# Block products of single chunks, with their weight sums on GpSimd, in a two-layer mLSTM and RG-LRU trunk

## The chip, the cores and the metric

The kernel runs on one core of a Trainium2 chip, in one launch. The metric is the device time of one execution in microseconds (us). Engines are named as in the profile: PE (TensorE matmul), PEld (its weight load), DVE (VectorE), ACT (ScalarE), POOL (GpSimd), SP (the queue that issues most DMAs).

## The reference

x is 256 tokens of 2048 channels, float32. Each of two layers does this; a final RMS norm follows.

```python
u = rms_norm(x, norm_g)
p = u @ w_in                               # 2048 x 12304
qk, v, o, z_a, ig, fg, xb, z_b = split(p)  # 2048 columns each, gates 8
qk = silu(causal_dwconv(qk, qk_conv))
h = mlstm_chunkwise(q, k, v, ig, fg)       # 8 heads
h = headwise_norm(h * sigmoid(o)) * head_norm_g
y_a = h * silu(z_a)
xc = causal_dwconv(xb, lru_conv_w) + lru_conv_b
y_b = rg_lru(xc, w_a, w_x, ...) * silu(z_b)   # 8 blocks of 256 x 256
x = x + concat([y_a, y_b]) @ w_out         # 4096 x 2048
```

Nearly all arithmetic is in the products with w_in and w_out; every weight is used once, for all 256 tokens.

## The kernel before

**Products in three passes.** A float32 weight is split into a high part wH (ACT casts to the float32r type) and the rest wL (DVE subtracts wH from the raw weight); activations are split likewise. A product is the sum of three matmuls: high by high, high by low, low by high. In the big products the activation (128 channels by 128 tokens) is the stationary operand and the weight, 512 columns wide, the moving one.

**Chunks, units and halves.** Columns are cut into four groups of 512 for each of qk, v, o, z, xb and zb. Such a chunk `("in", l, kind, g)` is four units, a unit two halves; a half is 128 x 1024 weights (512 KB), 2 blocks of 128 rows by 512 columns. It takes a load into `raw`, an ACT cast, a DVE subtraction (`prepare`, recorded at L114 like everything that goes through the helper `Behind`) and 12 matmuls in `mm_a` (L413). The out projection has four chunks of two units for each group; `gate` is one unit of small products (L879, 24 matmuls of 256 columns in a half).

**The order.** `_sequence` writes out the items of a layer group by group; the main loop walks the halves in that order. It loads into 8 buffers of `raw`, prepares halves up to `AHEAD` = 3 ahead of the matmuls (4 buffers each for wH and wL), and after each half lets the other work advance in the generators of `bg`. `pump` starts as much of it as an estimate of DVE's arrears (`st["lag"]`) allows; `require` forces it where a result is needed. `Behind` keeps other work of DVE and ACT behind the split that is due. Other work is: turning token layout into channel layout (`swapped`: a DVE transpose into `blk`, four SP transfers into `moved`, one POOL transfer back into `fr`), convolutions, attention, the recurrence, norms.

**Pairs.** In each layer two pairs of chunks (`PAIRS`: v and o of group 2; o and z of group 3) are done with seven products of blocks instead of eight: tokens, input channels and the two chunks are each halved, so that a block of weights is 1024 rows by the 512 columns of one chunk. A product is four halves of 6 matmuls of 512 columns (L1234 to L1236), in one bank of PSUM; results are put together in `res` by DVE. The 28 halves of a pair are spread between plain halves. Sums of activations are made by DVE in `sums` (`block_sums`); sums of weights are made in DRAM, by POOL transfers that copy and add (`weight_sums`, L1141), and are loaded from there; one product adds two loaded blocks on DVE.

**PSUM.** Two double banks `acc`, three single banks `aux` and one `bank` make the eight.

Of the kernel before, what the change touches and what calls it, by code (L numbers as in the profile page):

```python
# [16 lines left out]
P = 128  # L17
D = 2048
T = 256
# [8 lines left out]
AHEAD = 3  # L28
LANDING = 10.0
FAR = 15.0  # L30
BORDER = 7
BLANKS = 7
RATE = 0.9, 0.8
COPY, ADDING, TURN = 1.3, 2.6, 2.9
SLOTS = 8
SUMS_FROM = 20
# [7 lines left out]

def _sequence():


    def units(item):
        return [(item, j) for j in range(_nunits(item))]

    seq = []
    for l in range(DEPTH):
        for g in range(NG):
            fill = [("out", l, g - 1, c) for c in range(4)] if g > 0 else []
            head = {0: ("o", "qk", "v", "xb"), 1: ("qk", "o", "v", "xb"), 2: ("qk", "xb", "o", "v")}.get(g, ("qk", "v", "xb"))
            items = [("in", l, k, g) for k in head] + fill
            items += [("in", l, k, g) for k in (("o", "z") if g == NG - 1 else ("z",))] + [("gate", l, g)]
            items.insert(len(items) if g > 0 else -2, ("in", l, "zb", g))
            us = [u for it in items for u in units(it)]
            if l > 0 and g == 0:  # L60
                us[0:8] = [us[i] for i in (0, 4, 1, 5, 2, 6, 3, 7)]
            seq += us
        if l + 1 < DEPTH:
            u = [u for c in range(4) for u in units(("out", l, NG - 1, c))]
            seq += [u[i] for i in (0, 2, 1, 3, 4, 5, 6, 7)]
        else:
            seq += units(("last", l, NG - 1))
    return seq


PAIRS = (("v", NG - 2), ("o", NG - 2)), (("o", NG - 1), ("z", NG - 1))
PRODUCTS = 2, 2


def _blockwise(item):

    return item[0] == "in" and any(item[2:] in pair for pair in PAIRS[: PRODUCTS[item[1]]])

# [21 lines left out]
def tile_trunk(ctx, tc, x, xt, par, gw, gb, ws, final_g, out):  # L100
    nc = tc.nc
    G, PE = nc.gpsimd, nc.tensor
    done = {"wH": [], "wL": []}

# [15 lines left out]
    V, S = Behind(nc.vector, "wL"), Behind(nc.scalar, "wH")  # L120

    const = ctx.enter_context(tc.tile_pool(name="const", bufs=1))
    wraw = ctx.enter_context(tc.tile_pool(name="wraw", bufs=SLOTS))
    wsp = ctx.enter_context(tc.tile_pool(name="wsp", bufs=4))
# [5 lines left out]
    st = {"nload": 0, "lag": 0.0, "dma": 0.0, "t": 0.0, "rate": RATE[0], "nprep": 0, "pair": 0, "aux": 0}  # L130

    def aux(name):
        st["aux"] = (st["aux"] + 1) % 3
        return psum.tile([P, 512], F32, tag=f"aux{st['aux']}", name=name)

    def bank(name):
        return psum.tile([P, 512], F32, tag="bank", name=name)

    def new_acc():
        st["pair"] = 1 - st["pair"]  # L140
        return psum.tile([P, 2, 512], F32, tag=f"acc{st['pair']}", name="acc")
# [22 lines left out]
    def load_x_c(c):  # L164
        order(nc.sync.dma_start(out=xa(c), in_=xd[c]), st["ld"])
        st["dma"] += COPY

    def store_x(c):
        S.dma_start(out=xd[c], in_=xa(c))
        st["dma"] += COPY  # L170
# [86 lines left out]
    def lam_gen():  # L257
        lams = act.tile([P, 4, DEPTH, 16], F32, tag="res", name="lams")
# [11 lines left out]
    def order(ins, prev):  # L270
        tc.add_manual_dep(ins.ins, prev.ins.name,
                          mybir.DependencyInfo(mybir.DependencyClass.NoSync, mybir.DependencyReason.DATA),
                          reason="an order of the program")

    def paced(ins, prev):
        tc.add_manual_dep(ins.ins, prev.ins.name,
                          mybir.DependencyInfo(mybir.DependencyClass.Sync, mybir.DependencyReason.DATA),
                          reason="a transfer begun behind it")

    bg, aside = deque(), []  # L280
# [17 lines left out]
    def beside(g):  # L298
        aside.append(g)
        bg.append(g)  # L300
# [10 lines left out]
    def require(key):  # L311
        i = 0
        while key not in st:
            st["forced"] = True
            i = step(i)
# [19 lines left out]
    def load_half(hf):  # L335
        n = st["nload"]
        st["nload"] += 1
        if "from" in hf and hf["made"]:
            require(hf["made"])
        raw = hf["raw"] = wraw.tile([P, 1024], F32, tag="raw", name="raw")  # L340
        st["dma"] += COPY
        if "from" in hf:
            st["ld"] = nc.sync.dma_start(out=raw, in_=hf["from"])
            if "and" in hf:
                hf["other"] = wraw.tile([P, 1024], F32, tag="raw", name="raw")
                st["ld"] = nc.sync.dma_start(out=hf["other"], in_=hf["and"])
                st["dma"] += COPY
            return
        (item, j), i = hf["at"], hf["i"]
        if n < 8:  # L350
            w = 512 if n < 2 else 1024
            load_xt(n // 2, i)
            for o in range(0, 1024, w):
                nc.sync.dma_start(out=raw[:, o : o + w], in_=ws[blocks[item, j]][:, 1024 * i + o : 1024 * i + o + w])
        elif hf["paired"]:
# [3 lines left out]
        else:  # L359
            st["ld"] = nc.sync.dma_start(out=raw, in_=ws[blocks[item, j]][:, 1024 * i : 1024 * i + 1024])  # L360
# [3 lines left out]
    def add_unit(mms, before=None, after=None, paired=False, own=None):  # L364
        halves.append([dict(i=i, mm=mms[i], split=None, paired=paired, own=own and own[i],
# [1251 lines left out]
```

## Time and profile before

| | |
|---|---|
| median of 3 runs (lowest to highest) | 1478.68 us (1477.67 to 1482.82) |
| profiled execution, its time and its span | 1479.07 us, 1477.2 us |
| mean granted clock of TensorE | 0.999 |
| PE, DVE, ACT, POOL busy | 99%, 82%, 66%, 9% of the span |
| DMA | 417.06 MB, 282 GB/s on average |

In rows of the profile, a group of instructions is given as line, engine, operation, output<-inputs, output and input shapes, count, then busy us and mean ns of one, then the idle time of the engine before them and what ended it. A row of waits reads: who <- for whom: us in total, times, longest. A row of a timeline reads: start, length, engine, line, operation; rows of several instructions say so with x2. A row of a stretch reads: from, to, length, then busy us of an engine and the instructions in brackets. DMA rows give the count, the size and the median us from issue to landing.

### The profile page before, as it was taken

How to read it: one execution, taken by the hardware profiler on the slowest of the kernel's cores; microseconds unless marked ns; L12 is line 12 of the kernel's file. 1: busy time of each engine (PE TensorE's matmuls, PEld its weight loads, DVE VectorE, ACT ScalarE, POOL GpSimd, SP SyncE). 2: the span in 40 equal slices, each digit the busy share in tenths (PEclk: the TensorE clock that was granted, in tenths of full speed). 3: DMA queues.
4: the chain of work that ended last, by engine and by line, in shares of the span. 5: the costliest groups of instructions: out<-in, count | busy, mean ns of one | idle time of the engine just before them, and what ended most of it. 6: DMA issues, size and time to landing. Idle time of an engine off the chain costs nothing.

```text
span 1477.2 us, 19595 instructions
## 1 busy us (share of the span) xinstructions
PE 1460.8 (99%) x6734; PEld 1217.2 (82%) x6734; DVE 1213.1 (82%) x1710; ACT 981.5 (66%) x1255; POOL 129.5 (9%) x210
## 2 busy tenths in 40 slices
PE   9999999999999999999999999999999999999997
PEld 7888888888888888888888788888888788888885
DVE  6888898878888699888857789988787877998875
ACT  7666766568676666668665577655677756667774
POOL 0020110110100000100100201111000000000002
PEclk9999999999999999999999999999999999999999
DMA  9979999999989998988998888999988899888891
GB/s 343 337 242 283 284 315 292 309 252 330 348 288 257 289 335 286 303 250 285 293 301 258 229 277 275 292 299 275 316 263 295 251 261 286 307 287 269 232 342 60
DMA packets 158708, 417.06 MB, mean 282 GB/s; under 512 B 14848, under 2 KB 35344, under 8 KB 158608
## 3 DMA queue, kind: packets, MB, share of 16 engines
q1 hardware_dynamic: 136432, 340.01, 67.7%
q0 software_dynamic: 19712, 71.33, 21.1%
q10 hardware_dynamic: 2464, 4.47, 0.8%
q8 instruction: 53, 0.87, 0.2%
q14 instruction: 47, 0.39, 0.1%
HBM read 378.50 MB, written 74.99 MB: 307 GB/s over the span
## 4 chain that ended last, share of the span: by engine, by line
PE 86%; DMA 6%; DVE 4%; issue 3%; ACT 1%; SPq 0%; POOL 0%; POOLq 0%; DVEq 0%; ACTq 0%
PE acc L413 68%; PE ps_b L1234 3%; PE ps_b L1236 3%; PE ps_b L1235 3%; PE ps_gt L879 3%; DMA raw<-in_ws_dram 2%; DMA fr<-moved 2%; PE acc L426 2%; DMA moved<-blk 1%; DVE wL L114 1%; DVE xc L114 1%; DVE qc L114 1%; PE acc L1358 1%; PE acc L1359 1%; PE acc L1357 1%
## 5 line engine op out<-in xcount | busy, mean ns | idle before, releaser
L114 DVE TENSOR_TENSOR wL<-raw,wH 128x1024 fp32r<-128x1024 f32 (+1 forms) x580 | 692.8, 1202 | 187.1 <-ACT wH L114 185.2
L114 ACT CAST wH<-raw 128x1024 fp32r<-128x1024 f32 (+1 forms) x580 | 597.2, 1039 | 356.1 <-PE acc L413 250.2
L413 PE MATMUL acc<-wH,x_s 128*128 128x512 f32 x2496 | 783.7, 389 | 0.0
L413 PEld LDWEIGHTS acc<-wH,x_s 128*128 128x128 f32 x2496 | 468.3, 188 | 97.6 <-ACT wH L114 1.1
L413 PE MATMUL acc<-wL,x_s 128*128 128x512 f32 x1248 | 484.7, 389 | 3.0 <-DVE wL L114 3.0
L413 PEld LDWEIGHTS acc<-wL,x_s 128*128 128x128 f32 x1248 | 234.3, 188 | 51.9 <-DVE wL L114 4.1
L413 PE MATMUL acc<-wL,ybH 128*128 128x512 f32 x224 | 87.3, 390 | 0.6 <-DVE wL L114 0.6
L413 PE MATMUL acc<-wH,ybL 128*128 128x512 f32 x224 | 87.5, 390 | 0.3 <-DVE ybL L989 0.3
L413 PE MATMUL acc<-wH,ybH 128*128 128x512 f32 x224 | 87.6, 391 | 0.0
L413 PE MATMUL acc<-wH,yaH 128*128 128x512 f32 x224 | 87.4, 390 | 0.0
L413 PE MATMUL acc<-wL,yaH 128*128 128x512 f32 x224 | 87.2, 389 | 0.0
L413 PE MATMUL acc<-wH,yaL 128*128 128x512 f32 x224 | 87.2, 389 | 0.0
L114 ACT ACT_TABLE_LOAD x62 | 79.5, 1283 | 5.1 <-DVE qc L114 2.7
L1141 POOL DMA_DIRECT2D w_d<-in_ws_dram x64 | 48.9, 765 | 292.8 <-ACT wH L114 265.4
L536 POOL DMA_DIRECT2D fr<-moved x34 | 19.2, 566 | 511.3 <-DMA moved<-blk 450.9
L114 DVE SCALAR_TENSOR_TENSOR xc<-ch,pars,xc 128x255 f32<-128x255 f32 (+2 forms) x96 | 42.3, 477 | 10.3 <-ACT xc L114 10.0
L1234 PE MATMUL ps_b<-wH,sums 128*128 128x512 f32 x128 | 50.1, 391 | 0.0
L413 PEld LDWEIGHTS acc<-wH,ybL 128*128 128x128 f32 x224 | 42.1, 188 | 9.7 <-DVE ybL L989 1.0
L1236 PE MATMUL ps_b<-wH,sums 128*128 128x512 f32 x128 | 49.9, 390 | 0.0
L1235 PE MATMUL ps_b<-wL,sums 128*128 128x512 f32 x128 | 49.9, 390 | 0.0
L413 PEld LDWEIGHTS acc<-wL,ybH 128*128 128x128 f32 x224 | 42.1, 188 | 9.3 <-DVE wL L114 0.9
L413 PEld LDWEIGHTS acc<-wH,yaL 128*128 128x128 f32 x224 | 42.0, 188 | 8.8
(229 smaller groups left out, 1763.2 us busy)
## 6 DMA issues: line engine op xcount, KB each, us to landing
raw<-in_ws_dram SPq DMA_DIRECT2D x542, 512.0 KB, 6.7
w_d<-in_ws_dram POOLq DMA_DIRECT2D x64, 512.0 KB, 9.1
raw<-w_d SPq DMA_DIRECT2D x48, 512.0 KB, 6.7
fr<-moved POOLq DMA_DIRECT2D x34, 512.0 KB, 7.3
moved<-blk SPq DMA_DIRECT2D x132, 128.0 KB, 3.9
x_d<-stage POOLq DMA_DIRECT2D x24, 512.0 KB, 7.9
x_d<-x_acc ACTq DMA_DIRECT2D x8, 512.0 KB, 7.8
w_d<-w_d POOLq DMA_DIRECT2D x8, 512.0 KB, 7.0
```

The costliest lines, as they stand in the source:

```text
L114: ins = f(*a, **k)
L413: st["mm"] = PE.matmul(o, a_[:, kt, P * t : P * t + P], W[:, k], start=b, stop=z)
L426: PE.matmul(ps[:, ct, T * part : 2 * T], W[:, k, P * ct : P * ct + P], moving, start=first and k == 0 and part == 0, stop=last and k == 3 ...
L536: i0 = back.dma_start(out=fr.rearrange("p a c t i -> p a (c t i)"), in_=moved)
L879: PE.matmul(o, W[:, ib, jl], xs[:, ib, a, :], start=j == 0 and i == 0 and W is Hv and a == 0, stop=i == 1 and W is Lv, skip_group_check=True)
L1141: i0 = G.dma_start(out=wd[l][p][to][j][:, cs], in_=(wd[l][p][src][j] if src == 0 else block_unit(l, p, *src, j))[:, cs], **how)
L1234: PE.matmul(box["b"], aH, Hv[:, k], start=opening and k == 0, stop=False, skip_group_check=True)
L1235: PE.matmul(box["b"], aH, Lv[:, k], start=False, stop=False, skip_group_check=True)
L1236: PE.matmul(box["b"], aL, Hv[:, k], start=False, stop=kp == 3 and k == 1, skip_group_check=True)
L1357: PE.matmul(o, yH[:, kt, tsl], Hv[:, k, cs], start=start and k == 0, stop=False)
L1358: PE.matmul(o, yH[:, kt, tsl], Lv[:, k, cs], start=False, stop=False)
L1359: PE.matmul(o, yL[:, kt, tsl], Hv[:, k, cs], start=False, stop=stop and k == 1)
```

## The change

The pairs go, with their sums in DRAM. Blockwise now are single chunks: o and v of groups 1 to 3 and z of all groups, 10 chunks in each layer. Tokens, input channels and the 512 columns of one chunk are halved, so a block of weights is 1024 rows by 256 columns. A blocked half holds 128 rows of all four blocks (4 x 256 columns). GpSimd adds three more columns blocks beside them in SBUF:

```diff
+    def weight_sums(hf):
+        lo = hf["place"][0]
+        b = raws[:, lo : lo + 1792].rearrange("p (b n) -> p b n", b=7)
+        G.tensor_tensor(out=b[:, 4:6], in0=b[:, 0:4:3], in1=b[:, 1:2].to_broadcast([P, 2, 256]), op=ALU.add)
+        G.tensor_tensor(out=b[:, 6], in0=b[:, 4], in1=b[:, 3], op=ALU.add)
+        G.tensor_tensor(out=b[:, 1], in0=b[:, 6], in1=b[:, 2], op=ALU.add)
```

ACT and DVE then split 1792 columns, and the half does 7 products of 3 matmuls of 256 columns, for all seven block products at once, in two double banks that the chunk holds from its first half to its last:

```diff
+    def mm_s(l, box, kt):
...
+            for A, w, bank, at in ((x(0, 0), 0, a[:, 0], 0), (x(0, 1), 2, a[:, 1], 0), (s(1), 6, a[:, 1], 1),
+                                   (s(2), 5, b[:, 0], 0), (s(0), 4, b[:, 0], 1),
+                                   (s(3), 3, b[:, 1], 0), (x(1, 1), 1, b[:, 1], 1)):
+                o, cs = bank[:, 256 * at : 256 * at + 256], slice(256 * w, 256 * w + 256)
+                aH, aL = A()
+                PE.matmul(o, aH, H[:, cs], start=kt == 0 and at == 0, stop=False, skip_group_check=True)
+                PE.matmul(o, aH, L[:, cs], start=False, stop=False, skip_group_check=True)
+                st["mm"] = PE.matmul(o, aL, H[:, cs], start=False, stop=kt == 7, skip_group_check=True)
```

Behind the last half the blocks are joined, by one ACT copy and five DVE additions or subtractions, into a tile that shares its buffer with `tok`:

```diff
+    def joined_blocks(box):
+        st["held"].clear()
...
+        res = work.tile([P, 2, 512], F32, tag="tok", name="res")
...
+        S.copy(out=r[:, 3 * n : 4 * n], in_=a[:, 0, 0:n])
+        p1 = r[:, 3 * n : 4 * n]
+        tt_(r[:, 0 : 2 * n].rearrange("p (s n) -> p s n", s=2), p2_p6, p1.unsqueeze(1).to_broadcast([P, 2, n]), ALU.add)
+        tt_(r[:, 2 * n : 3 * n], r[:, n : 2 * n], p7, ALU.add)
+        tt_(r[:, n : 2 * n], p5, r[:, n : 2 * n], ALU.subtract)
+        tt_(r[:, 3 * n : 4 * n], r[:, n : 2 * n], p7, ALU.subtract)
+        tt_(r[:, n : 3 * n], r[:, n : 3 * n], p3_p4, ALU.add)
```

The sums of activations are made once a layer, in its first stretch, by GpSimd (three operations of 128 x 1024 for each of four sums) with an ACT copy and a DVE subtraction:

```diff
+        for i, p, q, op in ((0, x(1, 0), x(1, 1), ALU.subtract), (1, s(0), x(0, 0), ALU.subtract),
+                            (2, x(0, 0), x(1, 0), ALU.subtract), (3, x(0, 1), s(1), ALU.add)):
+            t_ = work.tile([P, 8, P], F32, tag="sE", name="sum_t")
+            for a, b, how in ((p(0), q(0), op), (t_, p(1), ALU.add), (t_, q(1), op)):
+                G.tensor_tensor(out=t_, in0=a, in1=b, op=how)
...
+            S.copy(out=sums[i][:, 0], in_=t_)
+            tt_(sums[i][:, 1], t_, sums[i].bitcast(F32)[:, 0], ALU.subtract)
```

The order is written anew: blocked halves alternate with plain ones, and two halves of the out projection go to one of z.

```diff
+            if g == 0:
...
+                seq += v + xb + mixed(z, zb) + gate
+            else:
+                fill = [h for c in range(4) for h in halves(("out", l, g - 1, c))]
+                seq += mixed(o, qk) + mixed(v, xb) + mixed(z, fill) + gate + zb
```

Buffers and queues: the raw weights lie in a ring `raws` of 7296 columns, the split ones in rings `highs` and `lows` of 4608 (a plain half takes 1024, a blocked one 1792). A load is issued when the halves that lay in its place have been split; sums are issued up to `SUMMED` = 5 halves ahead of the matmuls, splits up to 3 ahead where the ring has room. Everything that GpSimd issues, transfers too, now runs in program order (`InTurn`). In `swapped` the SP transfers are issued `SENT` = 2.5 us of the program's count after the transpose and the POOL transfer back `FETCHED` = 6 us after it, with one `fr` buffer for two; `moved` has six for two. The stage of an out projection, `res` and `tok` share one buffer. PSUM is three double banks `acc` and two single banks `aux`; the gates use an `acc`. The estimate of DVE's arrears counts 2.0 us for a blocked half and 1.2 for a plain one.

More of the change, by code (lines that the diff above doesn't have):

```diff
@@ L268, in lam_gen @@
         yield 1.5
[L270 to L280, printed above, removed]
+    bg = deque()
     timed = []
@@ L296, in pump, with beside @@
                 st["lag"] += c
-    def beside(g):
-        aside.append(g)
-        bg.append(g)
+    side = []
+    def beside():
+        for g in list(side):
+            try:
+                next(g)
+            except StopIteration:
+                side.remove(g)
     def before(t):
@@ L333, in tile_trunk, with load_half @@
     seq, blocks = _sequence(), _blocks()
[L335 to L348, printed above, removed]
+    def load_half(n, hf):
+        lo, hi = hf["place"]
+        raw = raws[:, lo : lo + 1024]
         (item, j), i = hf["at"], hf["i"]
+        src = ws[blocks[item, j]]
         if n < 8:
@@ L628, in gates_gen @@
         ts_(nG, Gm, -1.0, ALU.mult)
-        nc.gpsimd.dma_start(out=nG_d[l], in_=nG)
+        t0 = st["t"]
+        while before(t0 + SENT):
+            yield "wait"
+        G.dma_start(out=nG_d[l], in_=nG)
         sb = scs[0:64, 6, :]
@@ L669, in e_gen @@
         order(S.activation(out=E, in_=E, func=AF.Exp), st["wH"])
+        t0 = st["t"]
+        while before(t0 + SENT):
+            yield "wait"
         for h in range(2):
@@ L743, in gen @@
             yield from pause(g, 7.0, 3)
-            while any((k, l, g) not in st for k in ("E", "v", "so")) or st["ch"]:
+            while any((k, l, g) not in st for k in ("E", "v", "so")) or st["ch"] or g < NG - 1 and before(st["ch_t"]):
                 yield "wait"
@@ L772, in gen @@
             yield from pause(g, 7.0, 3)
+            while g > 0 and ("ybT", l, g - 1) not in st:
+                yield "wait"
             hh = work.tile([P, 2, 2, 256], F32, tag="sE", name="hh")
@@ L934, in zb_post @@
         ending = (l, g) == (DEPTH - 1, NG - 1)
-        fr = to_channels(l, acc, nc.sync if ending else G)
-        t0 = st["t"]
+        landed = to_channels(l, acc, nc.sync if ending else G)
         def gen():
-            while not ending and before(t0 + FAR):
+            while ("hz", l, g) not in st:
                 yield "wait"
-            while ("lru", l, g) not in st or ("hz" if ending else "yT", l, g) not in st:
-                yield "wait"
-            while st["turning"] or st["ch"]:
+            fr = yield from landed()
+            sg = work.tile([P, 4, T], F32, tag="sE", name="zsg")
+            S.activation(out=whole(sg), in_=pieces(fr), func=AF.Sigmoid)
+            tt_(whole(sg), whole(sg), pieces(fr), ALU.mult)
+            taken()
+            yield 0 if ending else 1.2
+            while ("lru", l, g) not in st or st["turning"] or st["ch"]:
                 yield "wait"
@@ L1026, in postfn @@
             if g < NG - 1:
[L1027 to L1031 removed]
+                stage = work.tile([P, 2, 512], F32, tag="tok", name="stage")
+                for t in range(2):
+                    S.copy(out=stage[:, t], in_=ps[:, t])
+                G.dma_start(out=xd[c], in_=stage, accum_op=ALU.add)
                 return
```

571 lines of the change are left out of this document (226 added, 345 removed).

## The prediction

> **What bounds the kernel now.** I read the page first: busy shares, then the slices.
>
> ```profile
> span 1477.2 us, 19595 instructions
> PE 1460.8 (99%) x6734; PEld 1217.2 (82%) x6734; DVE 1213.1 (82%) x1710; ACT 981.5 (66%) x1255; POOL 129.5 (9%) x210
> PE   9999999999999999999999999999999999999997
> DVE  6888898878888699888857789988787877998875
> ```
>
> A busy PE need not be a PE at its pace, so the pace comes from start times: the chain of waits (start, length) and the PE timeline.
>
> ```profile
> 49.17 54.43 PE acc L413 x240
> ```
> ```profile
> 144.90 0.40 PE L879 MATMUL ps_gt<-xcs,wH 128*128 128x256 f32 x2
> 145.13 0.28 PE L879 MATMUL ps_gt<-xcs,wL 128*128 128x256 f32 x1
> 145.25 0.40 PE L879 MATMUL ps_gt<-xcs,wH 128*128 128x256 f32 x2
> ...
> 177.73 0.39 PE L1234 MATMUL ps_b<-wH,x_s 128*128 128x512 f32 x1
> 177.96 0.39 PE L1235 MATMUL ps_b<-wL,x_s 128*128 128x512 f32 x1
> ```
>
> 240 matmuls of 512 columns in 54.43 us: 0.2267 us each, and the pairs' products step at the same pace. Of 256 columns three start within 0.35 us (144.90 to 145.25): 0.1167 each, so halving the columns nearly halves the time. The waits say how often PE stood still for its operands, and what the other engines wait for:
>
> ```profile
> DVE wL L114 <- ACT wH L114: 185.2, 155, 5.2
> ACT wH L114 <- PE acc L413: 250.2, 173, 5.4
> PE acc L413 <- DVE wL L114: 3.6, 3, 2.8
> POOL fr L536 <- DMA moved<-blk: 450.9, 28, 60.9
> ```
>
> PE lost 3.6 us to late splits; the split engines wait for PE. The kernel is bound by the number of matmuls, and DVE, 82% busy, is the nearest other limit.
>
> **The change part by part. PE.** 20 chunks (o and v of groups 1 to 3, z of all, two layers) become blockwise. Before, 8 of them ran in 4 pairs of 28 halves of 6 matmuls: 4 x 28 x 6 x 0.2267 = 152.3 us; 12 ran plain at 96 matmuls: 261.2. After: 160 halves of 21 matmuls of 256 columns, 160 x 21 x 0.1167 = 392.0. PE saves 21.5 us. The profiled execution took 1479.07 (1.87 outside its span; the median of the runs, 1478.68, is 0.4 lower, which I leave out). Floor: 1479.07 - 21.5 = 1457.6.
>
> **DVE and ACT splits.** A blocked half is split 1792 wide (4 blocks and 3 sums). By form:
>
> ```profile
> L114 DVE TENSOR_TENSOR wL<-raw,wH 128x1024 fp32r<-128x1024 f32 x564 | 681.7, 1217 | 183.9 <-ACT wH L114 182.0
> L114 DVE TENSOR_TENSOR wL<-raw,wH 128x512 fp32r<-128x512 f32 x16 | 11.0, 689 | 3.2 <-ACT wH L114 3.2
> L114 ACT CAST wH<-raw 128x1024 fp32r<-128x1024 f32 x564 | 587.4, 1051 | 352.5 <-PE acc L413 250.2 <-issue 16.3 <-PE ps_b L1236 13.4
> ```
> ```profile
> 828.49 2.35 DVE L114 TENSOR_TENSOR wL<-raw,wH 128x1024 fp32r<-128x1024 f32 x2
> ```
>
> Two splits back to back take 2.35, so one costs 2.35 - 1.22 = 1.14; 512 elements more cost 0.53, so 1792 cost 1.93 (2.01 alone). Splits before: 692.8 (all wL). After: 528 halves in all (264 in each layer), 368 plain and 160 blocked, 448 + 322 = 770, +77 for DVE; ACT in proportion 387 + 160 x 1.8 = 675 against 597 (all wH), +78, to some 73% busy: covered.
>
> The pairs' own DVE work goes:
>
> ```profile
> L114 DVE TENSOR_TENSOR raw<-raw 128x1024 f32<-128x1024 f32 x16 | 19.5, 1218 | 1.8 <-DMA raw<-in_ws_dram 1.8
> L114 DVE TENSOR_TENSOR res<-res,ps_b 128x512 f32<-128x512 f32 x20 | 13.5, 676 | 0.0
> L114 DVE TENSOR_TENSOR Pt<-ps_S,Pt 128x256 f32<-128x256 f32 x16 | 6.7, 416 | 0.0
> ```
> ```profile
> 0.00:1477.20 1477.20, 52.64 (x108) 1.00 0.90 282
> ```
> ```profile
> 0.00:1477.20 1477.20, 47.01 (x120) 1.00 0.90 282
> ```
>
> The last two are DVE's busy time on the tile sums and on sum_t over the whole span; they share instructions, so I take 80 for both with the forms that use res. Gone: 19.5 + 13.5 + 80 = 113. New: joining the products, 20 x 2.6 (two adds of 512 at 0.68, three of 256 at 0.42) = 52, and eight subtractions of 1.2 for the sums of x. DVE: 1213 + 77 - 113 + 62 = 1239, 85% of the floor. Alone it still fits.
>
> **GpSimd.** Per blocked half three adds (512, 256 and 256 elements), and per layer 12 adds of 1024 for the sums of x. The nearest rows, the last stage and two small operations:
>
> ```profile
> 1457.40 2.55 POOL L1378 TENSOR_TENSOR x_acc<-x_acc,fg 128x512 f32<-128x512 f32 x2 [0.82 <-ACT junk L114]
> ```
> ```profile
> L672 POOL TENSOR_SCALAR_AFFINE_SELECT E<-E x32: 282/283/1802, 98.6 to 1336.7; 128x128 f32<-128x128 f32 x32
> ```
> ```profile
> L647 POOL COPY at<-scs x16: 186/192/1285, 81.1 to 823.3; 32x16 f32<-32x16 f32 x16
> ```
>
> Two adds of 512 take 2.55: 1.25 each, and about 0.66 for 256, so 2.57 per half; 160 halves and 24 adds of 2.5 make about 470 us, on an engine that was 9% busy. It would be free if GpSimd ran beside DVE. The maxima above (1802 against 283, 1285 against 192) ask whether it does. DVE and POOL timelines at such places:
>
> ```profile
> 83.12 1.21 DVE L114 TENSOR_TENSOR wL<-raw,wH 128x1024 fp32r<-128x1024 f32 x1
> ```
> ```profile
> 83.30 1.09 POOL L647 COPY at<-scs 32x16 f32<-32x16 f32 x1
> ```
> ```profile
> 829.20 1.80 POOL L672 TENSOR_SCALAR_AFFINE_SELECT E<-E 128x128 f32<-128x128 f32 x1 [5.19 <-ACT E L114]
> ```
> ```profile
> 603.78 1.26 POOL L672 TENSOR_SCALAR_AFFINE_SELECT E<-E 128x128 f32<-128x128 f32 x3
> ```
> ```profile
> 604.83 1.29 DVE L114 TENSOR_TENSOR wL<-raw,wH 128x1024 fp32r<-128x1024 f32 x1
> ```
>
> The copy of 0.19 begun at 83.30 ends at 84.39, just behind the DVE split that ends at 84.33. The select of 0.28 begun at 829.20 sits out both splits of the 2.35 us row (they end at 830.84) and ends at 831.00. The other way round the split at 604.83 met the select that ended at 605.04 and took 1.29 instead of 1.22. In these rows the two engines do not read SBUF at once: each waits for the other's whole instruction. A DVE operation with one operand in PSUM is not held up:
>
> ```profile
> 1457.83 0.69 DVE L114 TENSOR_TENSOR x_acc<-x_acc,acc_x 128x512 f32<-128x512 f32 x1 [0.67 <-PE acc_x L1359]
> ```
>
> It ran inside the 2.55 us of the adds at its usual 0.69. The Trainium skill, "SBUF — State Buffer", section "Who interferes with whom", states this as a rule: a DVE instruction with two SBUF inputs and a GpSimd instruction that reads SBUF exclude each other for the whole instruction. The trace agrees (0.19 to 1.09, 0.28 to 1.80).
>
> So DVE and GpSimd share one budget. Pair (one blocked, one plain half): PE 21 x 0.1167 + 12 x 0.2267 = 5.17. Splits 1.93 + 1.14 = 3.07. Sums: 2.57, or 2.36 where the first 0.13 of each isn't held (830.84 to 831.00 is 0.15 for an operation of 0.28); I take 2.36, since a queue full on both sides hides that lead. Already 5.43. To this comes the other DVE work: (520 - 113) / 528 halves = 0.77 per half, 1.54 per pair, with the joining 1.87. Lower end: all of it elsewhere or beside GpSimd, 5.43, +0.26. Upper end: all of it counted, sums at 2.57, 7.51, +2.34. I take half of the 1.54, since the joining and the transposes have one SBUF input and some work moves to stretches without sums: 6.20, +1.03 per pair. There are 12 x 8 + 2 x 8 = 112 such pairs: +29, +115 taken, +262. With two plain halves to one blocked (z with the out projection, 48 triples; PE 7.89): 6.57, 7.72 taken, 9.41; 0, 0, +73. The sums of x, 2 x 30 us, fall among plain halves, where DVE leaves about 0.8 of each 2.72: 26 in 32 halves, so +4 per layer, +8.
>
> Sum: 1457.6 + 115 + 8 = 1580. Ends: 1487 and 1800; beyond 1660 only if nothing overlaps. With the skill's rule at full durations (2.01, 1.22, sums 2.7, three quarters of the other work) the sum would be about 1719.
>
> **DMA.** 72 sum transfers on POOL's queue and 64 loads of their results and seconds go; raw loads fall to about 528 of 512 KB. Raw storage is 7296 wide for 8192, about 5 halves ahead (13 us) against a landing of 6.7; PE covers it, so nothing.
>
> ```profile
> L1029 POOL DMA_DIRECT2D x_d<-stage x24 | 20.9, 872 | 251.8 <-ACT stage L114 251.8
> L114 ACT COPY stage<-acc 128x1024 f32<-128x1024 f32 x24 | 24.4, 1015 | 33.4 <-PE acc L413 33.4
> ```
> ```profile
> raw<-in_ws_dram SPq DMA_DIRECT2D x542, 512.0 KB, 6.7
> moved<-blk SPq DMA_DIRECT2D x132, 128.0 KB, 3.9
> x_d<-stage POOLq DMA_DIRECT2D x24, 512.0 KB, 7.9
> ```
> ```profile
> L413 PEld LDWEIGHTS acc<-wH,x_s 128*128 128x128 f32 x2496 | 468.3, 188 | 97.6 <-ACT wH L114 1.1
> ```
>
> **Waits and queues.** SP sends blk 2.5 us after the transpose, POOL fetches it 6 us after, when 3.9 of landing have passed; behind that fetch now stand the next sums, which run 5 halves ahead where the splits run 3, a cover of 5 us. Nothing, unless DVE runs late. Split storage is 4608 wide: two halves of lookahead beside a blocked one, not three. The result tile, the staging tile and tok share one buffer: in the six stretches with the out projection the last staging is freed some 10 us after PE (copy 1.2, issue 0.9, landing 7.9), while the joining of z wants it 2.5 us after. ACT then stands 7.5 us, and DVE's joining and split (2.6 + 1.1) end some 14 us after against 8.3 + 2.5 that the prepared halves cover: 0 to 3.4 us, six times; hidden in the bound above, 20 us without it.
>
> **The rivals.** (1) *Faster*: GpSimd fits into DVE's waits, which were 185 us for ACT alone. Then PE sets the time: 1458. It decides where a blocked half's sums hold DVE up by less than 5.17 - 3.07 - 1.54 = 0.56 us instead of 2.36. For it: DVE alone is at 85%; GpSimd's adds were never seen beside a DVE operation with two SBUF inputs, only its copies and selects. Against it: those waited without exception where a split was running. (2) *No change*: the shared reading costs little, and the shared buffer's 20 us eat the gain: 1478, from 1465 to 1500. Against it: 113 us of PE waits for wL need only 1 us per pair. (3) *The products do not pay*: a 256-column product with a changing weight tile costs more than 0.1167. The rows at 144.90 change it at every matmul too; at the 0.188 of one weight load (last row above) it would be +240, 1698. Very unlikely.
>
> **How the numbers follow.** Shared reading binds: 0.70, centre 1580, own range 1495 to 1660. Rival 1: 0.18. Rival 2: 0.11, nearly all of it within 0.5% (what a measurement here tells apart) or slower. Rival 3: 0.01. The 8-in-10 range must take in rival 1: 1458 to 1660. Faster 0.20 (rival 1 and a little of 2), same 0.09, slower 0.71.
>
> **What would show it.** Right: PE waits for wL of tens of us, in the o with qk and v with xb stretches; GpSimd adds of 512 far above 1.30, or splits of 1792 far above 2.01; PE starts 0.117 apart inside a half. Wrong: adds and splits at those durations side by side, PE idle under 30 us. A stall only behind the last staging would be rival 2.

## The result, and the profile after

The changed kernel takes 1944.67 us (median of four runs, 1940.47 to 1947.37): 1.314 times the time before, interval 1.3106 to 1.3176. The profiled execution took 1943.46 us. Slower was forecast, but 1580 us with a range up to 1660: the direction held and the size was missed by 365 us. The head of the page of the changed kernel:

```profile
span 1941.7 us, 22930 instructions
PE 1625.2 (84%) x8270; PEld 1353.5 (70%) x8270; DVE 1437.0 (74%) x1574; ACT 1055.0 (54%) x1256; POOL 849.8 (44%) x642
PE   9888877987889888987998677789877997879786
DVE  6888678866588677876878685688666786868764
PEclk9989889988899888998999888899889998889888
```

No engine is full over the span: PE stands at 84 %, DVE, which the forecast took for the new bound, at 74 %, and in no slice does DVE reach 90 %. That is the first sign that what was lost is waiting and not throughput. DVE's splits and GpSimd's sums by form (count, then busy us and mean ns of one, then the idle time ahead and what ended it):

```profile
L131 DVE TENSOR_TENSOR lows<-raws,highs 128x1024 fp32r<-128x1024 f32 x356 | 491.9, 1387 | 149.2 <-ACT highs L131 148.2
L131 DVE TENSOR_TENSOR lows<-raws,highs 128x1792 fp32r<-128x1792 f32 x160 | 344.9, 2159 | 186.1 <-ACT highs L131 185.8
L146 POOL TENSOR_TENSOR raws<-raws 128x512 f32<-128x512 f32 x160 | 272.9, 1706 | 509.8 <-DMA raws<-in_ws_dram 320.1 <-DVE lows L131 129.5 <-issue 17.6
L146 POOL TENSOR_TENSOR raws<-raws 128x256 f32<-128x256 f32 x320 | 419.9, 1312 | 25.1
```

Signs that the prediction named are there: the three adds of a half take 1.71 + 2 x 1.31 = 4.3 us where 2.57 was the price of GpSimd alone, a split of 1792 takes 2.16 instead of 2.01. The waits of the changed kernel (us in total, times, longest):

```profile
DVE lows L131 <- ACT highs L131: 338.2, 192, 10.1
POOL raws L146 <- DMA raws<-in_ws_dram: 320.1, 82, 13.0
ACT highs L131 <- POOL raws L146: 207.1, 73, 6.8
PE acc L460 <- DVE lows L131: 75.3, 69, 3.0
PE acc L459 <- ACT highs L131: 67.1, 27, 9.9
PE acc L437 <- DVE lows L131: 53.5, 43, 9.5
ACT res L131 <- DMA x_d<-stage: 46.1, 6, 8.4
PE acc L993 <- DVE res L131: 39.2, 7, 7.1
```

PE waited 3.6 us for late splits before; now it waits at every place where a weight is first used. The third line is the new one: ScalarE's cast waits for GpSimd's sums. One turn of that chain, from the timeline:

```profile
302.10 6.02 POOL L146 TENSOR_TENSOR raws<-raws 128x512 f32<-128x512 f32 x3 [10.13 <-DVE lows L131]
302.40 2.02 DVE L131 TENSOR_TENSOR lows<-raws,highs 128x1792 fp32r<-128x1792 f32 x1
...
305.77 1.75 DVE L131 TENSOR_TENSOR lows<-raws,highs 128x1024 fp32r<-128x1024 f32 x1
...
308.15 1.70 ACT L131 CAST highs<-raws 128x1792 fp32r<-128x1792 f32 x1 [4.29 <-POOL raws L146]
309.88 2.03 DVE L131 TENSOR_TENSOR lows<-raws,highs 128x1792 fp32r<-128x1792 f32 x1 [0.56 <-ACT highs L131]
...
311.96 0.38 PE L460 MATMUL acc<-lows,x_s 128*128 128x256 f32 x1 [1.40 <-DVE lows L131]
```

The three adds of one half (shown as one row of 6.02 us) begin only when a split of DVE has made room, 10.13 us after GpSimd ran out of work. They sit out the split of 302.40, and hold up the next one (1.75 us for 1.22). The cast of that half waits 4.29 us for them, DVE's split of it then comes 0.56 us after DVE was free, and PE waits 1.40 us for that split. The two engines exclude each other and also wait for each other's results; how much of the loss is the second, no run separates cleanly.

And what a wait costs beside itself, at another place. First the starts on PE, then the same stretch in windows (busy us of PE, PEld, DVE, ACT, POOL with counts; then PEclk, the granted clock):

```profile
612.82 0.28 PE L459 MATMUL acc<-highs,x_s 128*128 128x256 f32 x1
615.51 0.38 PE L460 MATMUL acc<-lows,x_s 128*128 128x256 f32 x1 [2.42 <-DVE lows L131]
...
616.05 0.42 PE L460 MATMUL acc<-lows,x_s 128*128 128x256 f32 x1
616.26 0.41 PE L461 MATMUL acc<-highs,x_s 128*128 128x256 f32 x1
...
619.25 0.29 PE L460 MATMUL acc<-lows,x_s 128*128 128x256 f32 x1
619.38 0.28 PE L461 MATMUL acc<-highs,x_s 128*128 128x256 f32 x1
```
```profile
612.00:615.50 3.50, 1.10 (x6) 0.64 (x4) 3.50 (x3) 2.83 (x5) 3.34 (x3) 1.00 0.29 94
615.50:619.25 3.75, 3.74 (x18) 3.74 (x19) 3.37 (x3) 1.06 (x2) 1.36 (x2) 0.55 0.80 147
619.25:623.00 3.75, 3.75 (x18) 3.08 (x18) 1.53 (x1) 2.19 (x2) 0.00 (x0) 1.00 0.83 194
```

Behind one wait of 2.42 us the granted clock of the next 3.75 us is 0.55 in the mean: until 619.25 matmuls of 256 columns start 0.21 apart instead of 0.117, and some 1.6 us more are gone. PE shows "busy" in that window.

From the start times of all matmuls the loss can be put into three heaps (my sums over the distances between starts, against 0.2268 us for 512 columns and 0.1167 for 256). Standing still: 367 us, against 12 before. Running at the halved clock behind a stall: 103, against 3. And a pace that is slower everywhere, 0.2342 for 4228 matmuls of 512 columns and 0.1179 for 3882 of 256: 31 + 5 = 36. The differences add up to 355 + 100 + 36 = 491; the measured time is 487 above the predicted floor of 1457.6. The experiments ask where the first heap comes from, and why the third exists at all.

### The profile page after: what moved, and what is told of

It is laid out like the page before. It is cut to its first block, busy times and chain, and to the rows that moved or that the text cites. A ratio compares the mean times of both kernels' runs of the same rounds, so it can differ in the third digit from the quotient of the medians.

```text
span 1941.7 us, 22930 instructions
## 1 busy us (share of the span) xinstructions
PE 1625.2 (84%) x8270; PEld 1353.5 (70%) x8270; DVE 1437.0 (74%) x1574; ACT 1055.0 (54%) x1256; POOL 849.8 (44%) x642
## 5 line engine op out<-in xcount | busy, mean ns | idle before, releaser
L131 DVE TENSOR_TENSOR lows<-raws,highs 128x1024 fp32r<-128x1024 f32 (+2 forms) x532 | 842.7, 1599 | 339.4 <-ACT highs L131 338.2
L131 ACT CAST highs<-raws 128x1024 fp32r<-128x1024 f32 (+2 forms) x532 | 645.6, 1228 | 551.1 <-POOL raws L146 207.1
L146 POOL TENSOR_TENSOR raws<-raws 128x256 f32<-128x256 f32 (+1 forms) x480 | 691.9, 1443 | 534.9 <-DMA raws<-in_ws_dram 320.1
L437 PE MATMUL acc<-highs,x_s 128*128 128x512 f32 x1728 | 583.7, 408 | 20.8 <-ACT highs L131 18.5
L437 PEld LDWEIGHTS acc<-highs,x_s 128*128 128x128 f32 x1728 | 336.8, 196 | 100.0 <-ACT highs L131 26.6
L437 PE MATMUL acc<-lows,x_s 128*128 128x512 f32 x864 | 354.2, 411 | 44.6 <-DVE lows L131 44.4
L437 PEld LDWEIGHTS acc<-lows,x_s 128*128 128x128 f32 x864 | 169.1, 196 | 93.1 <-DVE lows L131 58.8
L460 PE MATMUL acc<-lows,x_s 128*128 128x256 f32 x480 | 151.6, 316 | 75.6 <-DVE lows L131 75.3
L459 PE MATMUL acc<-highs,x_s 128*128 128x256 f32 x480 | 146.1, 304 | 74.0 <-ACT highs L131 67.1
L459 PE MATMUL acc<-highs,sums 128*128 128x256 f32 x640 | 194.7, 304 | 7.8 <-DVE res L131 5.7
L461 PE MATMUL acc<-highs,sums 128*128 128x256 f32 x640 | 192.0, 303 | 0.0
L460 PEld LDWEIGHTS acc<-lows,x_s 128*128 128x128 f32 x480 | 97.7, 203 | 104.4 <-DVE lows L131 101.3
L459 PEld LDWEIGHTS acc<-highs,x_s 128*128 128x128 f32 x480 | 97.3, 203 | 94.2 <-ACT highs L131 80.4
L459 PEld LDWEIGHTS acc<-highs,sums 128*128 128x128 f32 x640 | 134.9, 211 | 13.1 <-issue 7.6
L461 PE MATMUL acc<-highs,x_s 128*128 128x256 f32 x480 | 142.3, 296 | 0.0
L461 PEld LDWEIGHTS acc<-highs,sums 128*128 128x128 f32 x640 | 135.9, 212 | 0.0
L437 PE MATMUL acc<-highs,yaH 128*128 128x512 f32 x224 | 90.7, 405 | 12.0 <-ACT yaH L131 8.4
L437 PE MATMUL acc<-lows,yaH 128*128 128x512 f32 x224 | 90.8, 405 | 10.9 <-DVE lows L131 8.6
L461 PEld LDWEIGHTS acc<-highs,x_s 128*128 128x128 f32 x480 | 98.5, 205 | 0.5
```

The lines of the kernel that those rows point to most:

```text
L131: ins = f(*a, **k)
L146: ins = f(*a, **k)
L437: st["mm"] = PE.matmul(o, a_[:, kt, P * t : P * t + P], W[:, k], start=b, stop=z)
L459: PE.matmul(o, aH, H[:, cs], start=kt == 0 and at == 0, stop=False, skip_group_check=True)
L460: PE.matmul(o, aH, L[:, cs], start=False, stop=False, skip_group_check=True)
L461: st["mm"] = PE.matmul(o, aL, H[:, cs], start=False, stop=kt == 7, skip_group_check=True)
```

## The experiments

The theory in words: two-input DVE operations and GpSimd's adds exclude each other, and the sums stand in the weights' path. Its rivals: the loop of the raw ring (the sums wait for a landing, the landing for a free place, the place for the split: theory B), the short lead of the split ring, the buffer that stage, res and tok share, and GpSimd's own time whatever it reads. All kernels stand against the kernel before on the same chip.

**No weight sums**, all else as in the changed kernel.

```diff
-        G.tensor_tensor(out=b[:, 4:6], in0=b[:, 0:4:3], in1=b[:, 1:2].to_broadcast([P, 2, 256]), op=ALU.add)
-        G.tensor_tensor(out=b[:, 6], in0=b[:, 4], in1=b[:, 3], op=ALU.add)
-        G.tensor_tensor(out=b[:, 1], in0=b[:, 6], in1=b[:, 2], op=ALU.add)
+        pass
```

> Leaves out the weight sums on GpSimd (the three adds of each blocked half); ACT and DVE still split 1792 columns, of which three blocks hold old weights. Theory A (DVE and GpSimd reading SBUF exclude each other, and that sets the time): splits go back to 1.22 and 2.01 us, time 1460 to 1500. Theory B (the way of a half through the raw ring is a loop: load 4.8 us, sums 4.5, cast 1.7, subtraction 2.1, then the place is free again some five halves later; the loop's 13 us against 5 x 2.59 set the pace): without the 4.5 the loop is 8.6 us, time 1460 to 1500 too. Rival C (the shared buffer of stage, res and tok, the shorter split ring and the two aux banks cost most): stays above 1650.

Measured 1714.1 us, ratio 1.160 (1.155 to 1.165). The sums cost 231 us, and 256 us above the floor of 1457.6 are there without them. Theories A and B had both put this run at 1460 to 1500; only rival C (above 1650) had room for it.

**Write-only fills for the sums**, three or six to a half, issued at the same places; the cast waits for them as it does for the sums:

```diff
-        G.tensor_tensor(...)  # three
+        G.memset(b[:, 4:7], 0.5)  # three times, or six
```

> In place of the three adds GpSimd fills the three blocks three times with a constant (128 x 768 each time, about 0.73 us by the rate of the 128 x 832 fill, 0.79): it writes SBUF, reads none, some 2.2 us for a blocked half, and the split still waits for it. The sums are left out. Theory A: DVE is not held up, 1460 to 1500. Theory B: loop 4.8 + 2.2 + 1.7 + 2.0 = 10.7 us against 13, 1470 to 1550.

> As the run before with six fills: about 4.4 us of GpSimd for a blocked half, the 4.49 that the three adds took on average in the changed kernel, without reading SBUF. The sums are left out. Theory A: DVE is not held up, 1460 to 1520. Theory B: the loop is as long as in the changed kernel, 12.9 us, so 1750 to 1950.

Three fills: 1738.6 (1.177). Six: 1742.6 (1.171 to 1.188). Rows of the kernel with six:

```profile
L131 DVE TENSOR_TENSOR lows<-raws,highs 128x1024 fp32r<-128x1024 f32 x356 | 444.3, 1253 | 192.8 <-ACT highs L131 190.5 <-DMA moved<-blk 1.2
L131 DVE TENSOR_TENSOR lows<-raws,highs 128x1792 fp32r<-128x1792 f32 x160 | 323.5, 2025 | 92.9 <-ACT highs L131 92.1 <-DMA raws<-in_ws_dram 0.4
```
```profile
L146 POOL MEMSET raws<- 128x768 f32 x960 | 718.4, 751 | 247.8 <-DVE lows L131 194.6 <-DVE dn L131 7.0
```

GpSimd was as busy with fills (718.4 us) as with adds (718, each group of three from its first to its last), and 202 us of the 231 were gone; DVE's splits are back at 1253 and 2025 ns. The fills cost 28 (1742.6 against 1714.1), and half as many hardly less. They differ from the sums in two things, though: they read nothing, and so they need not wait for the load of their half either. ScalarE's cast, which waited 207.1 us for the sums, waits for six fills

```profile
ACT highs L131 <- POOL raws L146: 26.9, 22, 5.8
```

So the 202 us are the price of GpSimd reading loaded weights: the exclusion, and the place of the sums between the load and the cast. On the first of the two, the Trainium skill, "SBUF — State Buffer", section "Who interferes with whom", excludes a GpSimd instruction that only writes from the contention. This run agrees, with 1253 against 1387 ns for one split.

**The raw ring shorter**, 5632 columns for 7296:

```diff
-RAW, SPLIT = 7296, 4608
+RAW, SPLIT = 5632, 4608
```

> The changed kernel with a raw ring of 5632 columns for 7296: two pairs of halves for two and a half. Nothing left out. Theory A: the budget that DVE and GpSimd share is the same, 1940 to 2000. Theory B: the loop's 13 us now go round in four halves, 3.3 us and more for each against 2.6: 2200 to 2450.

1953.3 us (1.314 to 1.330), 9 more than the changed kernel. GpSimd's waits for the landings grew from 320.1 to 430.3 us and the cast's waits for the sums from 207.1 to 270.4, for these 9 us; theory B, with 2200 to 2450, falls here. That also speaks for a small part of the landings in the 202 us above, but does not measure it.

**Room for the splits, and a stage of its own**, each without sums, with the short raw ring to make place:

```diff
-RAW, SPLIT = 7296, 4608
+RAW, SPLIT = 5632, 5632
```
```diff
-RAW, SPLIT = 7296, 4608
+RAW, SPLIT = 5632, 4608
...
-                stage = work.tile([P, 2, 512], F32, tag="tok", name="stage")
+                stage = work.tile([P, 2, 512], F32, tag="stage", name="stage")
```

> As the run without weight sums (1714 us), with the split rings highs and lows of 5632 columns for 4608 (four halves for about three) and, for room, the raw ring of 5632, whose size moved nothing. The weight sums are left out; their places are filled once. Theory C1 (the split ring: a cast waits until PE is through a blocked half, and PE then waits for that split): 1714 falls by 80 to 160, to 1550 to 1630. Theory C2 (the buffer that stage, res and tok share, and joins that free their PSUM late): it stays at 1690 to 1720.

> As the run without weight sums (1714 us), with a buffer of its own for stage (raw ring 5632 for room, split rings as in the changed kernel). The weight sums are left out; their places are filled once. Theory C2: the six waits of res for the staged transfer (44.5 us) go, and with them some 20 us of a lowered clock behind them: 1640 to 1670. Theory C1: 1690 to 1720, other waits take their place.

The longer split ring: 1645.4 (1.107 to 1.120), 69 less than 1714.1. The waits of ScalarE's cast for PE (the ring is full until PE has read its oldest half) without sums, and then with the longer ring; L459 and L461, L435 and L437 are the same places of the two programs:

```profile
ACT highs L131 <- PE acc L459: 169.2, 93, 5.0
ACT highs L131 <- PE acc L435: 141.9, 113, 6.0
```
```profile
ACT highs L131 <- PE acc L437: 100.0, 75, 5.2
ACT highs L131 <- PE acc L461: 40.6, 36, 2.9
```

The stage of its own: 1678.9 (1.131 to 1.141), 35 less. What it removed is in the timeline of the changed kernel, behind one out projection:

```profile
1828.79 0.87 POOL L146 DMA_DIRECT2D x_d<-stage  x1 [7.42 <-ACT stage L131]
...
1839.32 0.37 ACT L131 COPY res<-acc 128x256 f32<-128x256 f32 x1 [8.39 <-DMA x_d<-stage]
1839.72 0.69 DVE L131 TENSOR_TENSOR res<-acc,res 128x512 f32<-128x512 f32 x1 [7.54 <-ACT res L131]
...
1840.56 0.77 PE L993 MATMUL acc<-xcs,highs 128*128 128x256 f32 x2 [7.12 <-DVE res L131]
```

The stage leaves for DRAM, and only when it has landed, at 1839.3, may the joining write res; and the gate's matmuls need the PSUM bank that the joining still reads. PE waits from the first moment, prepared splits or not.

**Room for the splits with the sums in place**:

```diff
-RAW, SPLIT = 7296, 4608
+RAW, SPLIT = 5632, 5632
```

> The changed kernel with its sums on GpSimd, split rings of 5632 and a raw ring of 5632; nothing left out. If the split ring and the shared reading add up, it gains as much as the run without sums does: 1944 falls to 1780 to 1860. If shared reading alone sets the time once the sums are there (theory A): 1900 to 1950.

1898.0 (1.279 to 1.291): 47 less than the changed kernel, and 253 more than the same rings without sums (1645.4). The sums do not become cheaper when the splits have more room.

**All of it**: no sums, long split ring, stage of its own, and two of the four sums of x, which frees the place:

```diff
-RAW, SPLIT = 7296, 4608
+RAW, SPLIT = 7296, 5632
...
+        sums = st["sums", l] = [act.tile([P, 2, 8, P], F32R, tag=f"xa{i}", name="sums") for i in range(2)] * 2
...
-        for i, p, q, op in ((0, x(1, 0), x(1, 1), ALU.subtract), (1, s(0), x(0, 0), ALU.subtract),
-                            (2, x(0, 0), x(1, 0), ALU.subtract), (3, x(0, 1), s(1), ALU.add)):
+        for i, p, q, op in ((0, x(1, 0), x(1, 1), ALU.subtract), (1, s(0), x(0, 0), ALU.subtract)):
```

> The changed kernel without weight sums, with split rings of 5632 and a buffer of its own for stage together; for room two of the four sums of activations are left out and the other two stand in for them (fewer GpSimd adds in the first stretch of a layer). If the causes add up: 1714 - 69 - 35 = 1610, less some 10 for the sums that are gone: 1590 to 1620. If one hides the other: 1640.

1558.5 (1.051 to 1.056), less than the 1590 to 1620 of the expectation. Of the 256 us without sums 156 are gone, 69 of them the ring's and 35 the buffer's by the runs above; what half the sums of x, the longer raw ring and the removal of all these together each have of the other 52 was not separated. Still 80 us slower than before.

**Idle work on GpSimd in the kernel before.** A tile that nobody reads and nobody waits for gets 159 times four fills, or 159 times the three adds; one raw buffer of eight makes room for it.

```diff
+        if n >= 20 and n % 7 in (0, 3):
+            for _ in range(4):
+                G.memset(idle[:, 0:3], 0.5)
```
```diff
+        if n >= 20 and n % 7 in (0, 3):
+            G.tensor_tensor(out=idle[:, 0:2], in0=idle[:, 2:4], in1=idle[:, 2:3].to_broadcast([P, 2, 256]), op=ALU.add)
+            G.tensor_tensor(out=idle[:, 1], in0=idle[:, 0], in1=idle[:, 2], op=ALU.add)
+            G.tensor_tensor(out=idle[:, 0], in0=idle[:, 1], in1=idle[:, 3], op=ALU.add)
```

> The kernel before, with one weight buffer fewer (7 for 8, for room) and, in two of seven halves, four constant fills on GpSimd (128 x 768, 0.755 us each, 3.0 together, 159 times) into a scratch tile that nobody reads. All theories: GpSimd writes only and no one waits, so 1477 to 1490; it is the measure for the next run.

> The run before with three adds (512, 256 and 256 elements, 2.7 us alone) in place of the four fills, 159 times, still on a scratch tile that nobody waits for. Theory A (a DVE operation with two SBUF inputs and a reading GpSimd operation exclude each other): splits average 1.30 and more for 1.22, GpSimd adds 4 us for 2.7, and time rises by 20 to 90 us over the run with fills. Without exclusion: the same as with fills.

Fills 1498.0 (1.011 to 1.016), adds 1820.4 (1.229 to 1.234). The 322 us between them are not the price sought: nothing paced the adds, so they ran one behind the other in the first 600 us, and transfers on GpSimd's queue stood behind them. PE's slices and a wait of ScalarE with the adds:

```profile
PE   7901834706587399999999999999999999999998
```
```profile
ACT ch L114 <- DMA fr<-moved: 141.4, 8, 84.8
```

Single gaps of PE of up to 76 us, and nothing lost once the adds had ended. The pair does not answer its question; the next one does.

**The same, paced**: each group is released by the cast of its own half.

```diff
-            G.tensor_tensor(out=idle[:, 0:2], ...)
+            paced(G.tensor_tensor(out=idle[:, 0:2], ...), st["wH"])
```

> The kernel before with seven raw buffers and 159 groups of four write-only fills of an idle tile on GpSimd that nobody reads, each group released only by the cast of its own half, so that they are spread over the whole run and no transfer queues behind more than one group. Both theories on the reading conflict: no reading, so 1480 to 1505 (the unpaced fills gave 1498).

> The same with 159 groups of the three adds of the changed kernel (512, 256 and 256 columns) in place of the fills, nobody waits for them, each group released by the cast of its own half. Theory 'throughput' (the adds take the shared read from VectorE, which has the slack of three split halves to make it good): 5 to 40 us over the fills. Theory 'exclusion by itself' (the adds cost what they cost in the changed kernel, some 200 us, whoever waits for them): about 1700. Between: the part of the 200 that needs no dependence of the weights on the sums.

Fills 1498.9 (1.013 to 1.019), adds 1628.4 (1.100 to 1.104): 129.5 us for the reading alone. (Both runs with fills cost some 20 us over the kernel before; a run further below also has seven raw buffers and loses nothing but pace, so the fills and not the buffer are the likely cause. The difference of adds and fills does not contain it.) The page's line of engines with fills and then with adds:

```profile
PE 1468.4 (98%) x6734; PEld 1221.0 (82%) x6734; DVE 1223.4 (82%) x1710; ACT 980.4 (66%) x1255; POOL 606.9 (41%) x847
```
```profile
PE 1513.8 (93%) x6734; PEld 1229.3 (76%) x6734; DVE 1457.5 (90%) x1710; ACT 976.2 (60%) x1255; POOL 831.1 (51%) x688
```

The splits in both, by form, and PE's wait for them with the adds:

```profile
L114 DVE TENSOR_TENSOR wL<-raw,wH 128x1024 fp32r<-128x1024 f32 x564 | 681.7, 1218 | 186.0 <-ACT wH L114 181.1 <-DMA moved<-blk 1.6 <-DMA raw<-in_ws_dram 1.5
```
```profile
L114 DVE TENSOR_TENSOR wL<-raw,wH 128x1024 fp32r<-128x1024 f32 x564 | 793.8, 1422 | 96.4 <-ACT wH L114 95.3
```
```profile
PE acc L416 <- DVE wL L114: 70.6, 54, 4.0
```

Here DVE is what the forecast said it would be: 90 % busy, its splits stretched from 1218 to 1422 ns, its waits for the cast halved, PE waiting for wL. The expected 5 to 40 us of slack was too little and the 200 of the other theory too much: with nobody waiting for the sums the reading costs 130 in the kernel before, with the weights waiting for them 202 to 253 in the changed one. That the waiting makes the difference fits the timeline at 302 us but is not shown by itself: the two kernels differ in their lead and their splits too.

**The sums on DVE itself**, issued three halves ahead instead of five. With five, in the rings of the changed kernel, this form ends in a deadlock and has no time.

```diff
-        G.tensor_tensor(...)  # three
+        tt_(...)  # the same three, on VectorE
...
-RAW, SPLIT = 7296, 4608
+RAW, SPLIT = 5632, 5632
-SUMMED = 5
+SUMMED = 3
```

> The changed kernel with the three adds on DVE (1.5 us for a blocked half, 245 us in all, issued 3 halves ahead for 5), split rings and raw ring of 5632; nothing left out. To be held against 1898 (same rings, adds on GpSimd) and 1645 (no adds). Theory A: DVE busy about 1272 + 245 = 1517 and no hand-over, 1720 to 1820. If exclusion costs nothing beyond its time: near 1898.

2016.4 (1.360 to 1.366), outside both expectations and worse than on GpSimd with the same rings (1898.0). The splits are undisturbed (1248 and 2025 ns), the adds cost DVE 244 us, and DVE is only 74 % busy. Its waits:

```profile
DVE lows L131 <- ACT highs L131: 372.0, 238, 6.6
ACT highs L131 <- DVE raws L131: 208.8, 84, 4.1
```

A half now goes through DVE, ScalarE and DVE again, in queues that run in order. It says nothing on the exclusion, since lead and order changed with it. It fits a chain with too little lead that sets the time while its engines have room, but does not show it.

**The lead by itself, in the kernel before**: three buffers for wH and wL instead of four, and preparing two halves ahead.

```diff
-AHEAD = 3
+AHEAD = 2
...
-    wsp = ctx.enter_context(tc.tile_pool(name="wsp", bufs=4))
+    wsp = ctx.enter_context(tc.tile_pool(name="wsp", bufs=3))
```

> The kernel before with three buffers each for wH and wL instead of four and a preparation two halves ahead instead of three, nothing else. It prices the step of the prediction that took the shorter lead of the changed kernel's split ring for free. Theory 'lead is free while no stage is saturated': 1478 to 1490. Theory 'the lead is what hides the bursts of VectorE's and ScalarE's other work': 30 to 80 us slower, 1510 to 1560.

1499.5 (1.013 to 1.017), 23 us slower: neither nothing nor 30 to 80. So the lead has a price even where DVE stands at 81 %. Why the same step is dearer in the changed kernel was not tested; its halves are uneven (1792 and 1024 columns), and bursts of other work may then be hidden less.

**The pace of 0.234.** In every kernel of the changed form so far, matmuls of 512 columns start 0.234 us apart at a full clock. The two programs keep the split weights at other addresses: wH and wL begin at 32 modulo 64 bytes, highs and lows at 0. Padding of 32 bytes moved the tiles of the kernel before (with seven raw buffers) to 0 modulo 64, and those of the run with all the room to 32 modulo 64; x_s kept its place modulo 64 in both, though not modulo 128 (32 instead of 96).

```diff
+    pad0 = ctx.enter_context(tc.tile_pool(name="pad0", bufs=1)).tile([P, 8], F32, name="pad0")
     wsp = ctx.enter_context(tc.tile_pool(name="wsp", bufs=4))
+    pad1 = ctx.enter_context(tc.tile_pool(name="pad1", bufs=1)).tile([P, 8], F32, name="pad1")
```
```diff
+    pads = [const.tile([P, 8], F32, name="pad0")]
     highs, lows = (const.tile([P, SPLIT], F32R, name=n) for n in ("highs", "lows"))
+    pads.append(const.tile([P, 8], F32, name="pad1"))
```

> The kernel before with seven raw buffers instead of eight and 32 bytes of padding ahead of the split tiles and 32 behind them, so that wH and wL begin at 0 modulo 64 bytes and x_s stays at 32 modulo 64. Theory 'address': the 512-column matmuls go from 0.227 to 0.234 apart, some 6100 x 7.4 ns = 45 us: about 1520 to 1525. Theory 'structure': the time stays within a few us of 1479 (seven raw buffers may cost up to 15), the pace at 0.227.

> The kernel of the run with room everywhere (no weight sums, 5632 columns of split ring, stage of its own, two of four x sums: 1558.5 us), with 32 bytes of padding ahead of highs and 32 behind lows, so that both tiles begin at 32 modulo 64 bytes per partition, as the split tiles of the kernel before do; x_s keeps its 32 modulo 64. Nothing else differs. Theory 'address': the 512-column matmuls of all kernels of the changed kind start 0.234 us apart instead of 0.227 because their moving operand begins at a multiple of 64; then the pace goes back to 0.227 and, with some 4400 such matmuls x 7.4 ns = 33 us, the time to about 1525. Theory 'structure' (the pace belongs to one big tile, or to the other traffic): pace and time stay at 0.234 and 1558.

The kernel before, moved (its split tiles lie 4064 bytes lower, a raw buffer of 4096 less and 32 more): 1510.0 us (1.020 to 1.023), 32 slower. In its chain of waits (start, length) stands the same stretch as in the prediction's second fence:

```profile
50.54 56.00 PE acc L415 x240
```

56.00 / 240 = 0.2333 where it was 54.43 / 240 = 0.2268; its 6052 matmuls of 512 columns at 6.5 ns each are 39 us, less 6 that PE idled less. No split comes late in it (PE waits 0.7 us for wL). Nor is it the seventh buffer: the kernel with paced fills has seven raw buffers too, but its idle tile takes the place of the eighth, so that the split tiles and x_s lie where they did, and the same stretch takes

```profile
49.68 54.43 PE acc L416 x240
```

as before. The other way the move gave little: 1550.7 (1.048 to 1.053) for 1558.5, with 232.7 ns for 512 columns and 118.7, slower than before, for 256. So the place of the tiles decides in the kernel before, but not by 32 modulo 64; in the changed one it moved the pace by 1.5 of 7.4 ns. The next pair put them at 96 modulo 128, where the kernel before has them: 96 bytes ahead and 32 behind, in the run with all the room and in the one with sums and the long split ring.

```diff
+    pads = [const.tile([P, 24], F32, name="pad0")]
     highs, lows = (const.tile([P, SPLIT], F32R, name=n) for n in ("highs", "lows"))
+    pads.append(const.tile([P, 8], F32, name="pad1"))
```

> The kernel of the run with room everywhere (1558.5 us) with 96 bytes of padding ahead of highs and 32 behind lows: both tiles then begin at 96 modulo 128 bytes, as wH and wL do in the kernel before (in the first padded run they began at 32 modulo 128, and its 512-column matmuls stood at 232 to 233 ns, between 227 and 234). Theory 'modulo 128': the pace goes to 0.227 and the time to about 1525 to 1530. Theory 'something else in the layout' (the blocks' own offsets, the distance between highs and lows): the pace stays at 0.231 or more and the time at 1545 or more.

> The changed kernel, complete, with a split ring of 5632 columns (raw ring 5632: 1898.0 us) and the same padding. Theory 'modulo 128': some 20 to 35 us less, about 1865 to 1880, as far as TensorE's own pace counts where it waits for the splits. Theory 'something else': 1890 to 1900.

1552.5 (1.049 to 1.053) and 232.7 ns again, and 1899.7 (1.284 to 1.289) against 1898.0 without padding. That it is the place modulo 128 falls; which rule of the place it is, and whether all of the slower pace in the changed kernel is one of place, stays open. Where the sums hold the kernel up a pace that is 1.5 ns better shows in no time at all.

No version here beats the kernel before: all that the products can bring is 21.5 us, and without any sums the best run is still 73 us slower.

## Why the prediction was wrong

What it had right: the floor's matmuls of 256 columns (0.1179 us each for 0.1167 where the clock is full, so rival 3 is out); the exclusion of DVE and GpSimd and that writes are free of it; DVE's own work without sums (1239 forecast, 1254 to 1282 measured in the runs without them); that GpSimd does not fit into DVE's waits (rival 1). Of its signs the late splits came (75.3 and 53.5 us of PE) and the stretched adds (1.71 us); the splits of 1792, 2.16 for 2.01, rose little.

What failed, term by term:

1. *"So DVE and GpSimd share one budget", +115 and +8.* The working priced a DVE that is saturated: the sum of durations against PE's time. With idle adds that nobody waits for this is what happens, and the price is 129.5. That it lies so near the 115 is in part luck: it was measured in the kernel before, whose splits and order are others, and the working itself has a slip. Sums of 2.57 of which 0.13 each is not held, three times, come to 2.18 and not 2.36; with that the pairs give 95 for 115, and the forecast 1560. In the changed kernel the sums are in the weights' path, DVE stands at 74 %, and the same adds cost 202 (against equally long fills) to 253 us (with the long ring), and the fills themselves 28 of the 231. The budget had no term for the time in which GpSimd waits for DVE's free place, ScalarE for GpSimd and DVE for ScalarE, as in the timeline at 302 us. Mechanism right, size wrong by a factor of about two; that these waits are the missing part is the likeliest reading, not a separate measurement.

2. *"Split storage is 4608 wide: two halves of lookahead beside a blocked one, not three"*: stated and given no price. It is worth 69 us without sums, 47 with them, and 23 for one buffer fewer in the kernel before. Its cover was PE's and DVE's mean load.

3. *The shared buffer, "0 to 3.4 us, six times", hidden in the bound.* The release of stage came as forecast: ScalarE waited 46.1 us in six waits, 7.7 each for the 7.5 of the working. But PE was thought to live on prepared halves meanwhile, while the next matmuls wanted the PSUM bank that res is made from: 39.2 us of PE in seven waits, 35 in the run that takes it away. The step overlooked who else holds what the joining reads.

4. *A wait costs its length.* Nothing was put down for the clock: running at half pace behind stalls cost 100 us more than before. Every one of the terms above carries its share of these.

5. *The pace of 512 columns was carried over*: 0.2268 before, 0.2342 after, some 36 us with the 256-column ones, more than the 21.5 that the products save. In the profile of before nothing shows it.

6. *"Raw storage ... so nothing"* held: 9 us for a quarter less. Of rival 2 the shared buffer was real, 35 us and a small part of the whole; that the shared reading costs little was wrong.

Together: of the 487 us above the floor the runs give 202 to the sums' reading (with their wait for the load), 28 to fills of the same length, 69 and 35 to ring and buffer, 52 to the sums of x, a longer raw ring and these together, and 101 are left in the run with all the room: by its starts 36 of pace, 53 of standing still beyond the 12 of before, and 15 of halved clock. These are differences of runs in one order of removal; in another order the shares would move, as the 47 for 69 shows.

## What to carry to other kernels

Work given to an engine that excludes another one has two prices: the time of the shared resource, which a sum of durations gives, and the waiting when each also needs the other's results, which it doesn't. Here the same adds cost 130 us where nobody waited for them and 202 to 253 where the weights did. When a change shortens a lead or lets two tiles share a buffer, follow the release to every holder, the PSUM bank too, and price it with the bursts of the engines and not with their means. Count what stalls cost in clock as well: 103 us here, beside 367 of standing still.

## What the runs showed of the hardware

- Where the operands lie in SBUF changes the pace of TensorE: 0.2268 us for 512 columns against 0.2333 with the split weights 4064 bytes lower and x_s 4032, at a mean granted clock of 0.998, 32 us of a run. Which of the two operands counts, and which addresses are the fast ones, was not found.
- Behind a single wait of 2.42 us the granted clock was 0.55 for 3.75 us. The Trainium skill, "TensorE: Matmul & The Clock Gate", section "HAM oscillation — how this bites in real kernels", warns of idle gaps above about 3.4 us; here a shorter one was followed by half clock, and the measurement decides. Not each was: of seven waits of 2.0 to 2.5 us in the changed kernel that had none above 0.4 in the 7 us before them, by the starts and the clock of its trace, three were.
- GpSimd's two-input adds take 1.25 to 1.3 us for 512 columns undisturbed and 1.71 to 1.88 in the mean beside DVE; DVE's split of 1024 goes from 1.22 to 1.42. Fills of 0.75 us on GpSimd leave DVE at 1.22.
